# A two-layer hybrid decoder trunk: the four products of the running sums go into one PSUM bank

## The chip, the cores and the metric

The kernel runs on one core of one Trainium2 chip. The metric is the device time of one execution in microseconds (us); lower is better. The engines are TensorE (PE in the profile; PEld is its weight load), VectorE (DVE), ScalarE (ACT), GpSimd (POOL) and SyncE (SP). Matrix products are written to PSUM, here eight banks of 128 x 512 float32, and are read from there by VectorE or ScalarE.

## The reference, cut to what matters

Two layers; 256 tokens, width 1024, everything float32. Each layer normalises the stream, multiplies it with one combined input weight, runs three token mixers side by side, projects and gates each, adds them, and applies one output projection.

```python
for layer in range(2):
    h = rms_norm(x, norm_w[layer])
    proj = jnp.einsum('bsd,de->bse', h, w_in[layer])
    (a_xbc, a_z, a_dt, b_q, b_k, b_v, b_z,
     c_q, c_k, c_v, c_f, c_z, gates) = jnp.split(proj, split_at, axis=-1)
    y_a = mamba2_branch(a_xbc, a_z, a_dt, ...)              # state space, 16 heads in 4 groups
    y_b = sliding_window_branch(b_q, b_k, b_v, b_z, ...)    # 16 heads, window 128
    y_c = forgetting_attention_branch(c_q, c_k, c_v, c_f, c_z, ...)
    branch = jnp.einsum('bsiw,iwd->bsid', jnp.stack([y_a, y_b, y_c], axis=2), w_proj[layer])
    g = jax.nn.sigmoid(gates.reshape(b, s, 3, d) + gate_bias[layer])
    x = x + jnp.einsum('bsd,de->bse', jnp.sum(g * branch, axis=2), w_out[layer])
return rms_norm(x, final_norm_w)
```

Two of the mixers need running sums over the tokens, and these are what the change touches:

```python
# state space: dt = softplus(dt_raw + dt_bias), a = -exp(a_log)
a_cum = jnp.cumsum(a_dt, axis=-1)                       # within each chunk of 128 tokens
seg = a_cum[..., :, None] - a_cum[..., None, :]
decay = jnp.where(causal, jnp.exp(jnp.where(causal, seg, 0.0)), 0.0)
# forgetting attention
log_f = jax.nn.log_sigmoid((f_logit + f_bias).astype(jnp.float32))
cum = jnp.transpose(jnp.cumsum(log_f, axis=1), (0, 2, 1))  # over all 256 tokens
sc = sc + cum[:, :, start:end, None] - cum[:, :, None, :end]
```

## The kernel before

**Dense products.** Every projection multiplies float32 numbers as a high part and a low part (`hi`, `lo`): three products per block of 128, high by high, low by high, high by low. The activations are split once. The weights come from DRAM on SyncE's queue into `raw` tiles of 128 x 1024, ScalarE copies the high part (L291) and VectorE subtracts for the low part (L292), one tile after the other, all the way through a layer. A projection's PSUM tile is evicted by ScalarE (L490, L491 and others) and the partial sums are added by GpSimd's accumulating transfer (L492) or by VectorE. All matrix products and transposes pass through two helpers, so the profile shows them under L107 and L111.

**PSUM.** Three of the eight banks form the pool `mm` (`pmm()`, L77), mainly for projections, five the pool `mx` (`pmx()`, L80), for everything else: scores, transposes, values, decays, running sums. A pool hands its banks out in a fixed rotation; whoever gets a bank waits until the last reader of its former content is done.

**Order.** The kernel's text is generated by a small planner: projections are the main stream, and the mixers are generators that are pumped between projections. A generator yields a number (microseconds of TensorE work until it is due) or a condition. The planner's order is the order in which each engine's queue receives its instructions; every engine runs its queue in order. Transfers of weights are issued on SP's queue, those of running sums on ScalarE's queue, the accumulating ones on GpSimd's.

**The sliding-window quads** (`attn_quad` with `window=True`, four heads at a time). Each takes four banks of `mx` for its scores. VectorE masks and finds the maximum of the first block (L619), ScalarE exponentiates (L614), then the second block: VectorE L627, L628, L632, ScalarE L614 reading PSUM directly. Then the denominators (L638 to L643), transposes of the probabilities `pp`, the copies L677, L679 and L680, and the products with the values, whose bank VectorE reads at L727 when the gate is multiplied in.

**The running sums** (`decay_logits`, L766). When the four logits tiles of a layer are there, it computes softplus and log-sigmoid on VectorE and ScalarE into `rates`, yields until due, and then multiplies with the triangle `tri` of ones:

- one product into a bank `pa` (128 tokens x 32) gives the state-space sums with tokens on partitions; ScalarE copies them to `acum` (L802),
- three products into a second bank `pc` (64 rows x 128 tokens, the last with `ones`, which carries the first chunk's total into the second) give both sums with tokens along the free axis; ScalarE copies them to `cum` (L811), and two transfers on ScalarE's queue (L814) store them in DRAM as `cumd`.

**Who reads the sums.** `cumd` is read back, broadcast to all partitions, by the forgetting attention (`bias`, L1036, then GpSimd's mask L1043) and by each of the four state-space groups (`bcg`, L860, on ScalarE's queue). A state-space group (`ssd_group`) subtracts `acum` (L872, L882), exponentiates on ScalarE (L873, L884, L888), multiplies with the products of B and C (L897) and runs the decay products on TensorE (L901 to L910). The convolution of the state-space input is elementwise: ScalarE L830, three VectorE L833, ScalarE L839, VectorE L840.

Of the kernel before, what the change touches and what calls it, by code (L numbers as in the profile page):

```python
# [13 lines left out]
AF = mybir.ActivationFunctionType  # L14
ALU = mybir.AluOpType

P = 128
# [31 lines left out]
def hybrid_trunk(  # L49
# [17 lines left out]
    def T(tag, shape, dtype=F32, bufs=None):  # L67
        count[0] += 1
        return sb.tile(shape, dtype, tag=tag, name=f"{tag}_{count[0]}",
                       bufs=bufs if bufs is not None else BUFS.get(tag, 1))  # L70

    def PS(tag, bufs):
        count[0] += 1
        return ps.tile([P, 512], F32, tag=tag, name=f"{tag}_{count[0]}", bufs=bufs)
# [4 lines left out]
    def pmx():  # L79
        return PS("mx", 5)  # L80

    act = nc.scalar.activation
# [18 lines left out]
    def mm(o, a, b, **kw):  # L101
        n = b.free_size()
        if a.dtype == F32R:
            clock["t"] += max(0.094, n / 2350.0)
        else:
            clock["t"] += max(0.2, n / 587.0) * (0.5 if a.free_size() == 64 or a.shape[0] == 32 else 1.0)
        nc.tensor.matmul(o, a, b, **kw)  # L107
# [82 lines left out]
    tri = T("tri", [P, P])  # L190
# [27 lines left out]
    def bc(ap, axis, n):  # L218
        s = list(ap.shape)
        s.insert(axis, n)  # L220
        return ap.unsqueeze(axis).to_broadcast(s)
# [204 lines left out]
    for l in range(L):  # L426
        y = Layer()
# [328 lines left out]
    def logits(y, t, i, p):  # L756

        if y.u is None:
            y.u = T("u", [P, 2, 32])
        o, b = y.u[:, t, 16 * i:16 * i + 16], y.hb[:, 16 * i:16 * i + 16]  # L760
        tt(o, p, b, op=ALU.add)
        y.logits += 1
        if y.logits == 4:
            launch(1, decay_logits(y), 0.0)

    def decay_logits(y):  # L766
        u = y.u

        tmp = T("L1", [P, 4, 2, 32])
        e = w = tmp[:, 0, :, :]  # L770
        act(e, u, AF.Abs)
        act(e, e, AF.Exp, scale=-1.0)
        s = tmp[:, 1, :, :]
        ts(s, e, 2.0, None, op0=ALU.add)
        nc.vector.reciprocal(s, s)
        tt(s, s, e, op=ALU.mult)
        s2 = tmp[:, 2, :, :]
        tt(s2, s, s, op=ALU.mult)
        q = tmp[:, 3, :, :].rearrange("p t c -> p (t c)")
        s2f = s2.rearrange("p t c -> p (t c)")  # L780
        sf = s.rearrange("p t c -> p (t c)")
        ts(q, s2f, 1.0 / 19.0, None, op0=ALU.mult)
        for m in (17, 15, 13, 11, 9, 7, 5, 3):
            stt(q, q, 1.0 / m, s2f, op0=ALU.add, op1=ALU.mult)  # L784
        stt(q, q, 1.0, sf, op0=ALU.add, op1=ALU.mult)
        q3 = q.rearrange("p (t c) -> p t c", t=2)
        y.dt = T("dt", [P, 2, 16])
        rates = T("rates", [P, 2, 2, 16])
        lf = tmp[:, 2, :, 0:16]
        ts(w[:, :, 0:16], u[:, :, 0:16], 0.0, 0.5, op0=ALU.max, op1=ALU.mult)  # L790
        tt(y.dt, w[:, :, 0:16], q3[:, :, 0:16], op=ALU.add)
        ts(y.dt, y.dt, 2.0, None, op0=ALU.mult)
        ts(w[:, :, 16:32], u[:, :, 16:32], 0.0, 0.5, op0=ALU.min, op1=ALU.mult)
        tt(lf, w[:, :, 16:32], q3[:, :, 16:32], op=ALU.subtract)
        ts(rates[:, :, 0, :], lf, -16.0, None, op0=ALU.mult)
        tt(rates[:, :, 1, :], y.dt, bc(y.nega, 1, 2), op=ALU.mult)
        yield D_CUM

        pa = pmx()
        mm(pa[:, 0:32], tri, rates[:, :, 1, :], start=True, stop=True)  # L800
        y.acum = T("acum", [P, 2, 16])
        act(y.acum, pa[:, 0:32].rearrange("p (t c) -> p t c", t=2), AF.Copy)  # L802


        pc = pmx()
        for c in range(2):
            mm(pc[32 - 32 * c:64 - 32 * c, 0:P], rates[:, c, :, :].rearrange("p w c -> p (w c)"), tri,
               start=True, stop=(c == 0))
        mm(pc[0:16, 0:P], rates[:, 0, 0, :], ones, start=False, stop=True)
        cum = T("L1", [64, P])  # L810
        act(cum, pc[0:64, 0:P], AF.Copy)  # L811
        y.cumd = dr.tile([2, 16, S], F32, name=f"cumd{y.l}", tag=f"cumd{y.l}")
        for c in range(2):
            nc.scalar.dma_start(y.cumd[:, :, c * P:(c + 1) * P].rearrange("w c s -> (w c) s"),  # L814
                                cum[32 - 32 * c:64 - 32 * c, :])
# [586 lines left out]
    with tc.manual_schedule(engines={ENG.PE, ENG.DVE, ENG.Activation, ENG.Pool}):  # L1402
# [11 lines left out]
        p = pmx()  # L1414
# [151 lines left out]
```

## Time and profile before

| | |
|---|---|
| median of 3 runs | 824.98 us (824.52 to 825.41) |
| the profiled execution | 824.13 us, of it 822.3 in the profile's span |
| granted TensorE clock, mean over the span | 0.994 |
| bytes moved | 170.35 MB, 207 GB/s on average |

How to read the lines that follow. The page gives for each engine its busy time, its share of the span and its instructions. A line of the waits reads: engine, tile and line that waited, what released it, then total us, count, mean us. A line of the timeline reads: start, duration, engine, line, operation, output <- inputs, sizes, count (several alike are merged into one line; the duration then is that of all of them), and in brackets the idle time ahead of it with what ended it. A line of the stretches reads: from and to, length, then for PE, PEld, DVE, ACT and POOL the busy us with the instructions that started, the granted TensorE clock (1.00 is full), the busy share of the 16 DMA engines, GB/s. Layer 0 lies roughly in the first half of the span, layer 1 in the second, and the running sums are formed at 118 to 125 and 511 to 518 us.

### The profile page before, as it was taken

The page shows a single profiled execution, that of the slowest core. Times are in us where ns is not written, and L with a number is a line of the kernel's source. Part 1 is how long each engine was busy: PE and PEld are TensorE (multiplying, and loading weights), DVE is VectorE, ACT ScalarE, POOL GpSimd, SP SyncE. Part 2 cuts the span into 40 slices and gives each one's busy share as a digit, 9 for nine tenths or more (in the row PEclk, how much of TensorE's full clock was granted, in tenths as well). Part 3 has the DMA queues.
Part 4 walks back from the last instruction along what each step waited for, and adds up shares of the span by engine and source line. Part 5 has one row for each costly group of instructions (what it writes and reads, how often), then busy time and mean ns, then how long its engine had stood idle before and what let it go on. Part 6 is the DMA issues. An engine that isn't in the chain of part 4 may idle for free.

```text
span 822.3 us, 14971 instructions
## 1 busy us (share of the span) xinstructions
PE 806.2 (98%) x5198; PEld 719.4 (87%) x5198; DVE 675.8 (82%) x1452; ACT 539.6 (66%) x1168; POOL 163.6 (20%) x233
## 2 busy tenths in 40 slices
PE   9999989999999999999999998999999999999996
PEld 8998968988888888888999897888888889888896
DVE  6878898979999797855786989897989877887665
ACT  7777767865776778543666776786557767684452
POOL 3066113120210111030005711302103110102100
PEclk9999999999999999999999999999999999999999
DMA  9898887688865554866689878668977556468632
GB/s 315 277 252 186 229 230 180 191 234 230 256 205 164 163 151 149 273 206 206 216 269 263 200 217 227 182 186 229 276 227 206 148 174 172 140 203 271 204 103 77
DMA packets 138708, 170.35 MB, mean 207 GB/s; under 512 B 9346, under 2 KB 106362, under 8 KB 138634
## 3 DMA queue, kind: packets, MB, share of 16 engines
q1 hardware_dynamic: 114960, 140.53, 55.2%
q0 software_dynamic: 12928, 12.63, 9.4%
q10 hardware_dynamic: 10746, 16.24, 6.4%
q8 instruction: 41, 0.67, 0.3%
q14 instruction: 33, 0.27, 0.1%
HBM read 154.63 MB, written 2.16 MB: 191 GB/s over the span
## 4 chain that ended last, share of the span: by engine, by line
PE 90%; DVE 6%; ACT 2%; issue 1%; DMA 0%; ACTq 0%; DVEq 0%
PE mm L107 80%; PE mx L107 7%; PE mx L111 4%; DVE lo L292 2%; DVE L L833 2%; ACT pp L614 1%; ACT hi L291 0%; DVE pp L619 0%; DMA L<-in_x_dram 0%; DVE pp L643 0%; DVE L L784 0%; DVE mx L627 0%; DVE L L727 0%; DVE L L840 0%; DVE L L680 0%
## 5 line engine op out<-in xcount | busy, mean ns | idle before, releaser
L107 PE MATMUL mm<-L,hi 128*128 128x512 f32 x1056 | 357.0, 389 | 0.0
L292 DVE TENSOR_TENSOR lo<-raw,hi 128x1024 fp32r<-128x1024 f32 (+2 forms) x276 | 312.0, 1149 | 53.8 <-ACT hi L291 50.9
L107 PE MATMUL mm<-hi,L 128*128 128x512 f32 (+2 forms) x1232 | 322.9, 351 | 0.1
L291 ACT ACTIVATE hi<-raw 128x1024 fp32r<-128x1024 f32 (+2 forms) x276 | 265.1, 981 | 63.3 <-PE mm L107 53.1
L107 PE MATMUL mm<-L,lo 128*128 128x256 f32 x1056 | 268.1, 274 | 0.0
L107 PEld LDWEIGHTS mm<-hi,L 128*128 128x128 f32 x1232 | 217.2, 190 | 24.0 <-issue 1.3
L107 PEld LDWEIGHTS mm<-L,hi 128*128 128x128 f32 x1056 | 196.2, 191 | 27.2 <-issue 4.1
L107 PE MATMUL mm<-lo,L 128*128 128x512 f32 (+2 forms) x616 | 213.6, 348 | 0.0
L107 PEld LDWEIGHTS mm<-L,lo 128*128 128x128 f32 x1056 | 203.7, 193 | 5.5
L107 PEld LDWEIGHTS mm<-lo,L 128*128 128x128 f32 x616 | 116.3, 190 | 11.7 <-DVE lo L292 0.2
L492 POOL DMA_DIRECT2D L<-L x68 | 59.5, 888 | 198.8 <-ACT L L491 132.3
L490 ACT ACTIVATE L<-mm 128x256 f32<-128x256 f32 x84 | 31.9, 379 | 25.9 <-PE mm L107 22.8
L833 DVE SCALAR_TENSOR_TENSOR L<-L,vec,L 128x255 f32<-128x255 f32 (+2 forms) x96 | 46.2, 481 | 2.0 <-ACT L L830 0.3
L1043 POOL TENSOR_SCALAR_AFFINE_SELECT bias<-bias 128x128 f32<-128x128 f32 x64 | 28.1, 476 | 87.4 <-DMA bias<-cumd 60.6
L1077 ACT ACTIVATE L<-L 128x512 f32<-128x512 f32 x24 | 15.1, 629 | 30.4 <-DVE L L1074 25.9
L656 ACT ACTIVATE pp<-pp,nm 128x128 f32<-128x128 f32 x64 | 28.2, 442 | 9.9 <-DVE nm L650 9.9
L492 POOL DMA_DIRECT2D qt<-L x16 | 13.8, 860 | 88.1 <-ACT qt L491 41.3
L614 ACT ACTIVATE pp<-pp,nm 128x128 f32<-128x128 f32 x32 | 12.6, 393 | 24.9 <-DVE nm L619 24.1
L964 POOL TENSOR_TENSOR sm<-sm,mhalf 128x4 f32<-128x4 f32 x8 | 9.9, 1241 | 88.0 <-DVE sm L961 88.0
L491 ACT ACTIVATE L<-mm 128x256 f32<-128x256 f32 x68 | 25.9, 380 | 1.0 <-DMA L<-L 1.0
L1122 POOL TENSOR_TENSOR L<-L,L 128x512 f32<-128x512 f32 x8 | 12.8, 1598 | 67.1 <-DVE L L1121 67.1
L928 ACT ACTIVATE L<-L 128x256 f32<-128x256 f32 x48 | 19.8, 413 | 9.3 <-DVE L L483 9.1
(210 smaller groups left out, 871.1 us busy)
## 6 DMA issues: line engine op xcount, KB each, us to landing
raw<-in_w_in_dram SPq DMA_DIRECT2D x191, 512.0 KB, 4.6
raw<-in_w_proj_dram SPq DMA_DIRECT2D x48, 512.0 KB, 5.5
L<-L POOLq DMA_DIRECT2D x72, 128.0 KB, 5.0
raw<-in_w_out_dram SPq DMA_DIRECT2D x16, 512.0 KB, 4.7
bias<-cumd ACTq DMA_DIRECT2D x16, 256.0 KB, 3.5
L<-cumd ACTq DMA_DIRECT2D x8, 512.0 KB, 5.8
L<-in_gate_bias_dram ACTq DMA_DIRECT2D x12, 256.0 KB, 4.5
qt<-L POOLq DMA_DIRECT2D x16, 128.0 KB, 5.2
```

The source lines that it names most:

```text
L107: nc.tensor.matmul(o, a, b, **kw)
L111: nc.tensor.transpose(o, a, i)
L291: keep(act)(hi, src, AF.Copy)
L292: keep(tt)(lo, src, hi.bitcast(F32), op=ALU.subtract)
L490: act(halves(lo), ordered(p[:, S:2 * S]), AF.Copy)
L491: last = act(halves(out), ordered(p[:, 0:S]), AF.Copy)
L492: nc.gpsimd.dma_start(out, lo, accum_op=ALU.add)
L614: act(pps[b][:, h // 2, h % 2 * P:h % 2 * P + P], of, AF.Exp, scale=0.125 if b else -1.0, bias=nm[:, e:e + 1], accum_out=sums[:, e:e + 1])
L656: act(pp[:, i, sl], pp[:, i, sl], AF.Exp, scale=-1.0, bias=nm[:, e:e + 1], accum_out=sums[:, e:e + 1])
L833: stt(a[:, s:S], x_[:, 0:S - s], y.vec[:, 16 * j + u:16 * j + u + 1], a[:, s:S], op0=ALU.mult, op1=ALU.add)
L928: act(th, o, AF.Tanh, scale=0.5)
L1043: nc.gpsimd.affine_select(out=bias[:, i, dst], in_=bias[:, i, src], compare_op=ALU.is_ge, fill=NEG, base=0, pattern=[[-1, P]], channel_mul ...
```

## The change

Only `decay_logits` changes. The pool `mx` is asked for one bank instead of two. The product for `acum` goes to the columns 128 to 159 of the bank whose columns 0 to 127 take the products for `cum`. ScalarE's copy to `acum` is written behind the last of the four products.

```diff
-        pa = pmx()
-        mm(pa[:, 0:32], tri, rates[:, :, 1, :], start=True, stop=True)
-        y.acum = T("acum", [P, 2, 16])
-        act(y.acum, pa[:, 0:32].rearrange("p (t c) -> p t c", t=2), AF.Copy)
-
-
         pc = pmx()
+        mm(pc[:, P:P + 32], tri, rates[:, :, 1, :], start=True, stop=True)
         for c in range(2):
             mm(pc[32 - 32 * c:64 - 32 * c, 0:P], rates[:, c, :, :].rearrange("p w c -> p (w c)"), tri,
                start=True, stop=(c == 0))
         mm(pc[0:16, 0:P], rates[:, 0, 0, :], ones, start=False, stop=True)
+        y.acum = T("acum", [P, 2, 16])
+        act(y.acum, pc[:, P:P + 32].rearrange("p (t c) -> p t c", t=2), AF.Copy)
         cum = T("L1", [64, P])
         act(cum, pc[0:64, 0:P], AF.Copy)
```

## The prediction

> **What bounds the kernel now.** I read the page first, for the engine that sets the end, then the list of who TensorE waited for, then the timeline and the stretches around its one long wait.
>
> ```profile
> span 822.3 us, 14971 instructions
> PE 806.2 (98%) x5198; PEld 719.4 (87%) x5198; DVE 675.8 (82%) x1452; ACT 539.6 (66%) x1168; POOL 163.6 (20%) x233
> ```
>
> TensorE works 806.2 of 822.3 us. Only 16.1 us are not its own work, so a gain can come from that remainder or from a faster clock. The waits of TensorE put half of the remainder in one place, twice, once per layer:
>
> ```profile
> PE mx L107 <- ACT pp L614: 8.0, 2, 4.0
> ...
> 118.36 0.30 PE L107 MATMUL mx<-rates,tri 128*128 128x32 f32 x2
> 122.18 0.37 ACT L614 ACTIVATE pp<-mx,nm 128x128 f32<-128x128 f32 x1 [0.40 <-DVE nm L632]
> 122.69 0.41 PE L107 MATMUL mx<-tri,rates 128*32 128x128 f32 x4 [4.02 <-ACT pp L614]
> 515.70 0.41 PE L107 MATMUL mx<-tri,rates 128*32 128x128 f32 x4 [4.03 <-ACT pp L614]
> ...
> 118.40:122.70 4.30, 0.28 (x5) 0.17 (x3) 4.23 (x21) 2.28 (x11) 0.00 (x0) 1.00 0.70 211
> 123.50:126.90 3.40, 3.40 (x12) 2.94 (x12) 3.24 (x8) 2.83 (x10) 0.86 (x1) 0.50 0.25 37
> ```
>
> These are exactly the products of the change. The product for `acum` (tile `pa`) runs at 118.36. The next one, for `cum` (tile `pc`), stands still until 122.69, because `pc` gets the bank of the first score of the running sliding-window quad, and L614's second-block exponential reads that bank until 122.55. TensorE's queue is in order, so everything behind it stands too. In the stretch 118.40 to 122.70 TensorE is busy 0.28 of 4.30 us and VectorE 4.23: VectorE is doing that quad's softmax and does not wait for TensorE. The last row shows a second cost: for 3.40 us after the wait the granted clock is 0.50.
>
> **The change, part by part.** It asks the `mx` pool once instead of twice. All four products then go into the bank that `pa` has now, and every later `mx` tile takes a bank one place earlier in the rotation of five, so one that was given back earlier or at the same time. The instructions and their order on each engine stay the same, transfers included; only the copy to `acum` falls behind the `pc` products, directly ahead of the copy to `cum`, and that is where ScalarE runs it in any case:
>
> ```profile
> 116.81 0.68 DVE L727 SCALAR_TENSOR_TENSOR L<-mx,L 128x512 f32<-128x512 f32 x1
> 117.81 0.68 DVE L727 SCALAR_TENSOR_TENSOR L<-mm,L 128x512 f32<-128x512 f32 x1
> 123.52 0.69 DVE L643 TENSOR_TENSOR pp<-pp,rsum 128x512 f32<-128x512 f32 x1
> 125.08 0.22 ACT L802 ACTIVATE acum<-mx 128x32 f32<-128x32 f32 x1
> 125.16 0.28 ACT L811 ACTIVATE L<-mx 64x128 f32<-64x128 f32 x1
> ...
> 123.25 0.59 PE L107 MATMUL mm<-L,hi 128*128 128x512 f32 x1
> 130.26 0.60 PE L111 MATMUL mx<-ident,pp 128*128 128x128 f32 x4
> 130.62 0.46 PE L107 MATMUL mm<-L,hi 128*128 128x512 f32 x1
> 135.94 0.60 PE L111 MATMUL mx<-ident,pp 128*128 128x128 f32 x4
> 516.43 0.80 PE L107 MATMUL mm<-L,hi 128*128 128x512 f32 x1
> 523.23 0.60 PE L111 MATMUL mx<-ident,pp 128*128 128x128 f32 x4
> ```
>
> *The wait.* The bank taken is free when the first L727 ends, 117.49, before `pa`'s product starts. So 4.02 and 4.03 us go. The projections behind start at 118.66 + 0.56 (122.69 to 123.25) = 119.22; the `mm` bank that the second L727 releases is back at 118.49. The next thing that could be late is the transposes of `pp`: they follow two projections later and need L643, which is done at 124.21.
>
> *The clock.* The two projections after the wait take 123.25 to 130.26 = 7.01 us; the next two, of the same work, 130.62 to 135.94 = 5.32. The half clock costs 7.01 - 5.32 = 1.69 us in layer 0, and 6.80 - 5.32 = 1.48 in layer 1. With no stand still I take it to go. So the transposes start at 119.22 + 5.32 = 124.54, after L643's 124.21. The Trainium skill ("TensorE: Matmul & The Clock Gate", section "What's actually happening") says that the clock halves after an idle window of about 3.4 us and comes back after as long a busy one; the trace agrees with 4.02 us of wait and 3.40 us at 0.50, and the two 1-2 us waits forecast below would leave the clock alone by it.
>
> *Copies.* `acum` and `cum` are copied at 125.08 and 125.16 although `pa` was done at 118.66: ScalarE has earlier work, which hides the `acum` copy's longer wait. Without that cover it would be 0.56 us late, and nothing reads `acum` before 175. Cost nothing.
>
> TensorE alone would so gain 4.02 + 1.69 + 4.03 + 1.48 = 11.22 us.
>
> **What catches it.** TensorE's operands come from the splits (L291 on ScalarE, L292 on VectorE) and the branches' elementwise work, and VectorE is at 82%. How much earlier does it get? It ran through the wait, so it can win only where it later idled for TensorE:
>
> ```profile
> 126.01 1.06 ACT L291 ACTIVATE hi<-raw 128x1024 fp32r<-128x1024 f32 x1 [0.57 <-PE mm L107]
> 127.84 0.38 ACT L490 ACTIVATE L<-mm 128x256 f32<-128x256 f32 x1 [0.77 <-PE mm L107]
> 130.46 0.38 ACT L490 ACTIVATE L<-mm 128x256 f32<-128x256 f32 x1 [0.41 <-PE mm L107]
> 132.21 1.06 ACT L291 ACTIVATE hi<-raw 128x1024 fp32r<-128x1024 f32 x1 [0.30 <-PE mm L107]
> ...
> 128.84 0.43 DVE L840 SCALAR_TENSOR_TENSOR L<-L,L 128x256 f32<-128x256 f32 x1 [0.51 <-ACT L L839]
> 130.09 1.23 DVE L292 TENSOR_TENSOR lo<-raw,hi 128x1024 fp32r<-128x1024 f32 x1 [0.49 <-ACT hi L291]
> 133.30 1.23 DVE L292 TENSOR_TENSOR lo<-raw,hi 128x1024 fp32r<-128x1024 f32 x1 [1.42 <-ACT hi L291]
> 134.70 1.00 DVE L833 SCALAR_TENSOR_TENSOR L<-L,vec,L 128x255 f32<-128x255 f32 x2 [0.17 <-ACT L L830]
> ...
> 127.00:134.70 7.70, 7.70 (x50) 7.09 (x49) 4.86 (x6) 5.97 (x15) 1.95 (x3) 1.00 0.58 129
> 134.70:167.60 32.90, 32.90 (x227) 28.75 (x227) 31.61 (x66) 24.96 (x59) 8.29 (x12) 1.00 0.81 220
> 520.00:527.67 7.67, 7.67 (x50) 7.07 (x49) 4.87 (x8) 6.36 (x15) 1.97 (x3) 1.00 0.55 122
> ```
>
> ScalarE idled 0.57 + 0.77 + 0.41 + 0.30 = 2.05 us for TensorE up to 132.21, VectorE 0.51 + 0.49 + 1.42 = 2.42 us for ScalarE up to 133.30. With TensorE 5.7 us ahead both run without these gaps. Since each feeds the other I take 2.2, between the two. After 134.70 VectorE has 31.61 us of work in 32.90: it can win at most the other 1.29 there, which is mostly short hand-overs with ScalarE, so I count none of it. Layer 1 has the same picture (4.87 against 4.86 us busy). The bounds for VectorE's lead are therefore 0 (every gap filled by something else) and 2.42 + 1.29 = 3.71.
>
> Where does TensorE meet VectorE? At the decay products of the first state-space group:
>
> ```profile
> 167.57 0.42 ACT L839 ACTIVATE L<-L 128x256 f32<-128x256 f32 x1 [1.65 <-DVE L L833]
> 167.62 0.33 ACTq L860 DMA_DIRECT2D L<-cumd  x1
> 175.13 0.16 DVE L872 TENSOR_TENSOR ds<-L,acum 128x4 f32<-128x4 f32 x1 [4.19 <-DMA L<-cumd]
> 187.67 0.33 ACTq L860 DMA_DIRECT2D L<-cumd  x1
> 192.68 0.16 DVE L872 TENSOR_TENSOR ds<-L,acum 128x4 f32<-128x4 f32 x1 [1.98 <-DMA L<-cumd]
> 193.93 1.88 DVE L897 TENSOR_TENSOR L<-L,mx 128x512 f32<-128x512 f32 x3
> 195.24 1.53 PE L107 MATMUL mx<-L,L 128*64 128x128 f32 x24
> 586.14 1.88 DVE L897 TENSOR_TENSOR L<-L,mx 128x512 f32<-128x512 f32 x3
> 588.21 1.53 PE L107 MATMUL mx<-L,L 128*64 128x128 f32 x24
> ```
>
> The broadcast of L860 is issued at 167.62 behind ScalarE's L839, which waited for VectorE. VectorE then waits for its landing (175.13). The next one is issued at 187.67 and ends at 192.68; its group's three L897 end at 195.81, and TensorE uses the last of them some two thirds into the pass that starts at 195.24, at 196.26. So this chain keeps VectorE's lead of 2.2 and no more, and TensorE may lead it by another 196.26 - 195.81 = 0.45 us. In layer 1: 588.21 + 1.02 - (586.14 + 1.88) = 1.21. TensorE keeps 2.2 + 0.45 = 2.65 us in layer 0 and 2.2 + 1.21 = 3.41 in layer 1, and gives back 5.71 - 2.65 = 3.06 and 5.51 - 3.41 = 2.10 in new waits, some of it possibly at earlier meetings. After each meeting both engines are ahead together and nothing takes it back.
>
> *Sum.* 2.65 + 3.41 = 6.06 us. The profiled execution took 824.13 us (span 822.3 and 1.8 around it), so 818.07; the median of the runs is 824.98, 0.85 above it, so 818.9. With the bounds of VectorE's lead: 2 x 0 + 1.66 = 1.66 gives 823.3, and 2 x 3.71 + 1.66 = 9.08 gives 815.9.
>
> **Rivals.**
>
> *TensorE keeps everything.* The broadcasts land as much earlier as their data exist: `cum` leaves TensorE 4 us sooner, and the transfers of the wait's aftermath move little (share 0.25, 37 GB/s). Then 824.98 - 11.22 = 813.8. Against it: L860's issue at 167.62 waits for VectorE, not for `cum`, and 31.61 of 32.90 leaves VectorE no room for 5.7 us.
>
> *VectorE wins nothing,* 823.3: the gaps of 0.49 and 1.42 could belong to the loads of `raw`, which slow to 37 GB/s just there. Against it, the rows name TensorE as what ScalarE waited for.
>
> *The clock falls again: slower.* TensorE gives back 5.16 us in several new waits. If each of them, though short, halved the clock as the 4.02 us one did, each would cost another 1.6 us (mean of 1.69 and 1.48). From four such waits on the 6.06 is eaten; three a layer give 818.9 + 9.6 = 828.5. The places are the pass at 195.24, that at 588.21 and projections ahead of them that wait for VectorE. For it: the one long wait did cost that. Against: the new ones are under 2 us each, and TensorE works without a gap on either side. The Trainium skill has this rule: in "TensorE: Matmul & The Clock Gate", "A second HAM failure mode: psum-queue depth-cycling", frequent small idles between groups of matmuls keep the clock swinging; no row of this trace shows it for idles of this size.
>
> *The change does not do what it says:* if the shared bank were handed out at `pc`'s place, the wait for L614 would stay and the time be 825.0. The rotation speaks against it: the first request takes the bank of L727.
>
> **How the numbers follow.** The forecast has 0.65, TensorE keeping all 0.17, VectorE winning nothing 0.08, the clock falling again 0.05, no effect 0.05. The predicted time is 818.9. The forecast's own range is 815.9 to 821.3 (half of VectorE's lead lost: 2.2 us). To hold 8 in 10 I take 813.6 to 822.4: it takes in the rival at 813.8 and most of the way to 823.3. What a measurement can tell from no change is about 0.2%, 1.65 us. VectorE winning nothing lies on that bound, so half of it counts as the same: faster 0.65 + 0.17 + 0.04 = 0.86, same 0.09, slower 0.05.
>
> **What would show it.** The wait of `mx` for L614 gone from TensorE's waits; clock 1.00 where the projections follow `cum`'s products; the first transposes of `pp` near 124.5 and 517.7. VectorE's L833 that starts now at 134.70 near 132.5, and its L872 at about 173 instead of 175.13. New TensorE waits of together about 5 us, named after VectorE's L897 or splits, between 150 and 200 and again around 588. It would be wrong if L872 is 5 us earlier (then near 813.8), or not at all (823.3), or if rows at clock 0.50 appear behind the new waits.

## The result, and the profile after

| | before | after |
|---|---|---|
| median | 825.19 us (824.52 to 825.97, 4 runs) | 817.61 us (816.47 to 818.14, 4 runs) |
| ratio, after to before | | 0.9906, 95% interval 0.9889 to 0.9923 |
| profiled execution, its span | 824.13, 822.3 | 816.47, 814.7 |
| mean granted TensorE clock | 0.994 | 0.999 |

The change takes 7.6 us off. The prediction was 818.9 us, 6.1 off; the measured median lies 1.3 us below it. The edit shortens the file by three lines, so L830, L833, L839, L860, L872 and L897 of the text above are L827, L830, L836, L857, L869 and L894 in profiles of the change.

First the page of the changed kernel, and who TensorE waited for. The three numbers of a line of the waits are the total in us, the times, and the longest single wait (not the mean):

```profile
span 814.7 us, 14971 instructions
PE 805.0 (99%) x5198; PEld 717.2 (88%) x5198; DVE 675.2 (83%) x1452; ACT 538.2 (66%) x1168; POOL 162.6 (20%) x233
...
PE mx L111 <- POOL ident masks.py:199: 1.5, 1, 1.5
PE mm L107 <- ACT qt L491: 0.7, 1, 0.7
PE mx L107 <- DVE L L894: 0.5, 2, 0.4
```

The wait for L614 is gone from the list. The work is the same. TensorE's idle time fell from 16.1 to 9.7 us and its busy time, in which the half clock counted, by 1.2. Two new lines are there, for an eviction (L491) and for the decay products (L894), 1.2 us in all.

The timeline and one stretch around the running sums of layer 0, and the sums and the next transposes in layer 1:

```profile
118.48 0.30 PE L107 MATMUL mx<-rates,tri 128*128 128x32 f32 x2
118.72 0.41 PE L107 MATMUL mx<-tri,rates 128*32 128x128 f32 x4
124.62 0.60 PE L111 MATMUL mx<-ident,pp 128*128 128x128 f32 x4
...
506.81 0.30 PE L107 MATMUL mx<-rates,tri 128*128 128x32 f32 x2
507.05 0.41 PE L107 MATMUL mx<-tri,rates 128*32 128x128 f32 x4
512.95 0.60 PE L111 MATMUL mx<-ident,pp 128*128 128x128 f32 x4
...
119.20:124.60 5.40, 5.40 (x34) 4.92 (x33) 5.09 (x26) 4.06 (x21) 0.00 (x0) 1.00 0.42 129
```

All four products run in one go, the projections behind them at clock 1.00. From the first product for `cum` to the transposes of `pp` it is now 124.62 - 118.72 = 5.90 us, and in layer 1 the same. Before it was 130.26 - 122.69 = 7.57 and 523.23 - 515.70 = 7.53: the half clock had cost 1.67 and 1.63.

Then the places at which VectorE's chain ties TensorE down. These are VectorE's convolution at the point where it had stopped idling, ScalarE's issues of the broadcast, and VectorE's first use of it:

```profile
132.27 1.00 DVE L830 SCALAR_TENSOR_TENSOR L<-L,vec,L 128x255 f32<-128x255 f32 x2
165.17 0.33 ACTq L857 DMA_DIRECT2D L<-cumd  x1
171.85 0.17 DVE L869 TENSOR_TENSOR ds<-L,acum 128x4 f32<-128x4 f32 x1 [3.36 <-DMA L<-cumd]
184.40 0.33 ACTq L857 DMA_DIRECT2D L<-cumd  x1
188.16 0.17 DVE L869 TENSOR_TENSOR ds<-L,acum 128x4 f32<-128x4 f32 x1 [0.72 <-DMA L<-cumd]
...
553.47 0.33 ACTq L857 DMA_DIRECT2D L<-cumd  x1
561.10 0.16 DVE L869 TENSOR_TENSOR ds<-L,acum 128x4 f32<-128x4 f32 x1 [4.30 <-DMA L<-cumd]
578.00 0.16 DVE L869 TENSOR_TENSOR ds<-L,acum 128x4 f32<-128x4 f32 x1 [1.29 <-DMA L<-cumd]
```

VectorE's lead in layer 0 is 134.70 - 132.27 = 2.43 us, and the issue has the same lead, 167.62 - 165.17 = 2.45. Up to here it is close to the forecast 2.2. But then L869 is 175.13 - 171.85 = 3.28 us early, and the second one 192.68 - 188.16 = 4.52. The broadcasts landed faster: issue to use 6.68 us in place of 7.51, and 3.76 in place of 5.01.

TensorE's own lead can be read off at four points (before against after): transposes of layer 0, 130.26 against 124.62, 5.64 us; first product of the sums in layer 1, 511.38 against 506.81, 4.57; transposes there, 523.23 against 512.95, 10.28; the whole execution, 824.13 against 816.47, 7.66. So layer 0 won 5.64 and gave back 1.07; layer 1 won 5.71 and gave back 2.62. The row of before for 511.38:

```profile
511.38 0.30 PE L107 MATMUL mx<-rates,tri 128*128 128x32 f32 x2
```

TensorE's instructions and their order are the same in the two kernels, so its lead can be followed product by product. It falls at four places in each layer: at a bank that VectorE's L1071 reads, at one that VectorE's L727 reads, at one that ScalarE's L491 evicts, and at the decay products behind L894. The two large falls are in layer 1. Its rows, of the changed kernel, and under them the row of before that belongs to 563.13 (the lead falls there from 571.46 - 561.80 = 9.66 at the transposes ahead of it to 571.81 - 563.13 = 8.68):

```profile
561.29 0.21 ACT L870 ACTIVATE ds<-ds 128x4 f32<-128x4 f32 x1 [3.04 <-DVE ds L869]
561.80 0.60 PE L111 MATMUL mx<-ident,L 128*128 128x128 f32 x4
563.13 0.48 PE L107 MATMUL mm<-L,hi 128*128 128x512 f32 x1 [0.73 <-ACT qt L491]
579.99 1.04 PE L107 MATMUL mx<-L,L 128*64 128x128 f32 x12 [0.36 <-DVE L L894]
581.19 0.88 PE L107 MATMUL mx<-L,L 128*64 128x128 f32 x12 [0.16 <-DVE L L894]
```

```profile
571.46 0.60 PE L111 MATMUL mx<-ident,L 128*128 128x128 f32 x4
571.81 0.46 PE L107 MATMUL mm<-L,hi 128*128 128x512 f32 x1
```

The first row shows that ScalarE, too, stood 3.04 us for the first reader of the broadcast (its exponential of `ds`), and its evictions with it.

### The profile page after: what moved, and what is told of

It is laid out like the page before. It is cut to its first block, busy times and chain, and to the rows that moved or that the text cites. A ratio compares the mean times of both kernels' runs of the same rounds, so it can differ in the third digit from the quotient of the medians.

```text
span 814.7 us, 14971 instructions
## 1 busy us (share of the span) xinstructions
PE 805.0 (99%) x5198; PEld 717.2 (88%) x5198; DVE 675.2 (83%) x1452; ACT 538.2 (66%) x1168; POOL 162.6 (20%) x233
## 4 chain that ended last, share of the span: by engine, by line
PE 81%; DVE 10%; DMA 3%; ACT 3%; issue 3%; ACTq 0%; DVEq 0%
PE mm L107 72%; PE mx L107 6%; PE mx L111 3%; DVE lo L292 3%; DMA L<-cumd 3%; DVE L L830 2%; ACT hi L291 1%; ACT pp L614 0%; DVE L L292 0%; ACT L L827 0%; DVE pp L643 0%; DVE L L894 0%; DMA L<-in_x_dram 0%; DVE pp L619 0%; DVE L L679 0%
## 5 line engine op out<-in xcount | busy, mean ns | idle before, releaser
L830 DVE SCALAR_TENSOR_TENSOR L<-L,vec,L 128x255 f32<-128x255 f32 (+2 forms) x96 | 46.2, 481 | 1.7
L614 ACT ACTIVATE pp<-pp,nm 128x128 f32<-128x128 f32 x32 | 12.6, 394 | 23.5 <-DVE nm L619 22.7
L491 ACT ACTIVATE L<-mm 128x256 f32<-128x256 f32 x68 | 25.9, 381 | 0.7 <-DMA L<-L 0.7
```

The source lines that it names most:

```text
L491: last = act(halves(out), ordered(p[:, 0:S]), AF.Copy)
L830: stt(a[:, s:S], x_[:, 0:S - s], y.vec[:, 16 * j + u:16 * j + u + 1], a[:, s:S], op0=ALU.mult, op1=ALU.add)
```

## The experiments

The question after the result was what took back 3.7 of the 11.35 us that TensorE won, and whether the half clock was a cost of its own. The theory: VectorE, standing still for the landing of the broadcast with splits queued behind it. The main rival: VectorE's own work, or ScalarE's evictions, hold TensorE in any case.

**The wait of VectorE taken away.** In the change and, beside it, in the kernel before, the first reader of the broadcast is held behind the last of the `xdt` products (L866 in the changed kernel, L869 in the kernel before):

```diff
-            tt(xdt[:, t, :].rearrange("p (h d) -> p h d", h=4),
+            ready = tt(xdt[:, t, :].rearrange("p (h d) -> p h d", h=4),
...
-        tt(ds, bcg[:, :, P - 1], y.acum[:, 0, hs], op=ALU.subtract)
+        with tc.issue_after(ready.ins): tt(ds, bcg[:, :, P - 1], y.acum[:, 0, hs], op=ALU.subtract)
```

> The change, with VectorE's first reader of the broadcast (the subtraction into ds, L869) held behind L866, some 10 us later in VectorE's queue; TensorE's order is the same. Theory that VectorE stands still for the broadcast's landing with splits queued behind it, and that this is what takes back the rest of TensorE's lead: VectorE's waits for the broadcast (3.4, 0.7, 4.3 and 1.3 us) go, TensorE's lost lead behind 163 us and 554 us (1.0 and 2.4 us) mostly with them, and the time is 814 to 815.5. Rival, that VectorE's own work or ScalarE's evictions hold TensorE: the waits go or move and the time stays at 817 to 818.

> The kernel before with the same late L872. Theory: there TensorE was not held by VectorE behind its long wait (no wait for L897 or for a split in its trace), so VectorE's freedom is worth nothing: 825 us, within 0.2%. Rival, that VectorE's wait for the broadcast already cost time in the kernel before: 822 to 823.

> The change once more, beside the next two on the same chip: 817.6 us. The landing of the first group's broadcast (issue to L869's start) was 6.7 us in layer 0 and 7.6 in layer 1; if such times vary from execution to execution, they differ here by up to 1 us, and the time with them.

Measured on one chip: the change again 816.80 us (816.17 to 816.98, 4 runs; ratio 0.9892, 0.9876 to 0.9909), the change with the late reader 814.94 (814.76 to 814.97; ratio 0.9871, 0.9857 to 0.9886), the kernel before with the late reader 825.56 against 825.34 (ratio 1.0005, 0.9996 to 1.0015). In the timeline of the change with the late reader, L869 stands without a bracket, so it waits for no landing, and TensorE's two new waits of the changed kernel have left its list. The first row is of the timeline, the rest are TensorE's waits:

```profile
178.25 0.25 DVE L869 TENSOR_TENSOR ds<-L,acum 128x4 f32<-128x4 f32 x1
...
PE mx L111 <- POOL ident masks.py:199: 1.5, 1, 1.5
PE mx L111 <- DMA L<-in_x_dram: 0.5, 1, 0.5
PE mm L107 <- DVE L L1071: 0.2, 1, 0.2
```

In the same stretch of 40 us in layer 1, VectorE gets from 33.72 to 37.04 us of work and TensorE from 38.72 to 39.97. The row of the changed kernel comes first:

```profile
546.00:586.00 40.00, 38.72 (x239) 32.91 (x238) 33.72 (x60) 23.84 (x47) 8.80 (x13) 1.00 0.88 245
```

```profile
546.00:586.00 40.00, 39.97 (x249) 34.68 (x248) 37.04 (x68) 25.87 (x49) 9.22 (x13) 1.00 0.93 267
```

The same edit brings 1.9 us behind the change and nothing in the kernel before, where TensorE had no wait for a split or a decay product to lose. This version is also the fastest of all. TensorE's lead over the profiled execution of before shows where the gain lies. In the table stands how much of it is lost at each of the four places, layer 0 and layer 1, in us (lines of the changed kernel):

| place | the change | the change again | the change, late reader |
|---|---|---|---|
| bank read by VectorE L1071 | 0.36, 0.33 | 0.38, 0.33 | 0.39, 0.28 |
| bank read by VectorE L727 | 0.30, 0.30 | 0.30, 0.29 | 0.29, 0.29 |
| bank evicted by ScalarE L491 | 0.06, 0.99 | 0.51, 0.77 | 0, 0 |
| decay products behind L894 | 0.36, 0.98 | 0.91, 0.38 | 0, 0 |

So the theory holds for the larger part: the losses at L491 and L894, 2.4 to 2.6 us, go with the wait for the landing. The other 1.3 us are lost in all three, at banks that VectorE's own work frees late; for them the rival is right.

**The half clock alone.** The time in which TensorE stands still is filled with useless products; nothing else changes. The second kernel has `range(8)`:

```diff
         mm(pa[:, 0:32], tri, rates[:, :, 1, :], start=True, stop=True)
+        for _ in range(17):
+            nc.tensor.matmul(pa[:, P:2 * P], tri, ident, start=True, stop=True)
```

> The kernel before with 17 more products of tri and ident, written into unused columns of pa's bank, in the time in which TensorE waits for L614 (about 3.7 of 4.0 us filled). Theory that the clock falls because TensorE stands still: granted clock 1.00 behind the wait, the two projections there in 5.3 us instead of 7.0, and since 1.7 and 1.5 us of lead are less than TensorE could keep, all of it in the time: about 822.0 us. Rival, that the half clock costs nothing in the end because VectorE is not ahead: about 825. If the clock falls for another reason than the idle time: 0.50 stays and 825.

> As filled_wait, with 8 products in place of 17: they take about 1.9 us (17 took 4.0), so TensorE stands still for about 2.1 us. If the clock falls only behind a stand still nearly as long as the 4.0 us one, it stays 1.00 and the time is that of filled_wait, about 821.5. If 2 us are enough, 0.50 stands behind the wait and the time is 824 to 825.

Filled: 821.46 us against 824.55 (821.09 to 821.77, 5 runs; ratio 0.9961, 0.9947 to 0.9975). The timeline shows the products, the `cum` product at its old place, and the stretch behind it at full clock:

```profile
118.57 4.04 PE L802 MATMUL mx<-ident,tri 128*128 128x128 f32 x34
122.75 0.41 PE L107 MATMUL mx<-tri,rates 128*32 128x128 f32 x4
...
123.30:126.90 3.60, 3.60 (x23) 3.33 (x23) 3.39 (x10) 2.65 (x12) 0.86 (x1) 1.00 0.23 32
```

So the wait itself is still paid, but the half clock behind it is not: 3.1 us, close to the 1.67 + 1.63 = 3.30 that it cost in the profile. The clock fell because TensorE stood still, and its cost reaches the time in full.

Half filled gave no single answer: 823.06 us (821.90 to 824.97, 10 runs; ratio 0.9979, 0.9970 to 0.9989). The profiled execution, the fastest, kept the clock in both layers. Its timeline and the stretch behind the wait:

```profile
123.49 0.41 PE L107 MATMUL mx<-tri,rates 128*32 128x128 f32 x4 [2.15 <-ACT pp L614]
...
123.00:126.50 3.50, 3.01 (x21) 2.60 (x22) 3.19 (x13) 3.24 (x16) 0.86 (x1) 1.00 0.16 56
```

Two other executions of it had a mean clock of 0.994, as the kernel before has, and 824.67 and 824.97 us. By these mean clocks a stand still of 2.15 us sometimes costs the clock and sometimes not; no fallen execution of this kernel was profiled.

**Which reader holds the bank.** In the kernel before, the product for `acum` takes a bank of the other pool:

```diff
-        pa = pmx()
+        pa = pmm()
```

> The kernel before with pa's product in a bank of the pool mm, so that cum's products get the bank of L727 without a wait. Theory that only the last reader of the bank counts: the wait for L614 goes, but every projection gets a later bank of mm: the second one behind the products needs the bank of the projection ahead of them, which ScalarE evicts only at 124.0 to 124.4 (L490, L491), and would wait from about 122.0, 2.4 us, in each layer. If the clock holds through that, TensorE is 1.6 + 1.7 us ahead behind it, less than VectorE lets it keep: about 818.5 to 819; if it falls, 1.6 us, about 822. Rival, that two banks at that place cost the 4 us whichever pool gives them: 825.

820.02 us against 824.67 (819.82 to 821.31, 4 runs; ratio 0.9942, 0.9926 to 0.9959). The wait for L614 is gone, and the forecast wait for the eviction is there, in both layers. Behind the second one the clock fell:

```profile
124.82 0.48 PE L107 MATMUL mm<-L,hi 128*128 128x512 f32 x1 [2.40 <-ACT L L491]
514.76 0.48 PE L107 MATMUL mm<-L,hi 128*128 128x512 f32 x1 [2.43 <-ACT L L491]
...
123.00:126.50 3.50, 1.68 (x10) 1.57 (x11) 3.19 (x11) 3.50 (x15) 0.86 (x1) 1.00 0.04 13
515.00:519.00 4.00, 4.00 (x16) 3.47 (x16) 3.93 (x8) 3.92 (x10) 1.74 (x2) 0.59 0.28 42
```

Two banks do not cost 4 us by themselves. What costs is the last reader of the bank that one gets. The time lies between the two cases expected, as the clock fell in one layer of the profiled execution and held in the other.

**The rotation.** The change, and one more bank asked for behind the shared one and left unused:

```diff
+        pmx()
         cum = T("L1", [64, P])
```

> The change, with one bank of the mx pool asked for and left unused behind the shared one, so that every later tile gets the bank that it had before. Theory that the shared bank alone is the gain: 817.6 us, as the change. Rival, that the later tiles' earlier banks carry part of it: between 818.5 and 825, with new waits for L614 or L643 in front of the transposes of pp.

816.83 us (816.63 to 817.18, 4 runs; ratio 0.9903, 0.9888 to 0.9918), by its ratio as the change (0.9906 and 0.9892). The later tiles' earlier banks are worth nothing that can be measured.

**One layer at a time.** The edit is the change under `if y.l == 0:` or `if y.l == 1:`, with the old lines in the other branch.

> One shared bank in layer 0, two banks in layer 1. The trace of the change puts 4.6 us of the gain in layer 0: about 820.6 us against 825.2 before. If layer 0 is worth what the prediction's step gave it (2.65 us), 822.5. In layer 1 the wait of 4.0 us for L614 and the half clock behind it stay.

> Two banks in layer 0, one shared bank in layer 1. The trace of the change puts 3.1 us there: about 822.1 us. The prediction's step gave 3.41 us: 821.8. If the two layers' gains depend on each other, the two single gains do not add up to 7.6 us.

Layer 0 alone: 821.13 us (820.59 to 821.31, 4 runs; ratio 0.9954, 0.9939 to 0.9969), 3.4 us off. Layer 1 alone: 821.39 (820.79 to 821.66; ratio 0.9957, 0.9942 to 0.9972), 3.2 off. The two make 6.6 us, against 7.7 for both together on the same chip (824.55 - 816.83, of the kernel with the old rotation, as the change itself did not run there). The profiles show one reason: in the layer that keeps the wait, the clock stayed low for longer than in the profiled execution of before. The first pair of lines is layer 1 of the one kernel, the second pair layer 0 of the other:

```profile
511.79 0.64 PE L107 MATMUL mx<-tri,rates 128*32 128x128 f32 x4 [4.01 <-ACT pp L614]
520.19 0.60 PE L111 MATMUL mx<-ident,pp 128*128 128x128 f32 x4
```

```profile
123.08 0.64 PE L107 MATMUL mx<-tri,rates 128*32 128x128 f32 x4 [4.02 <-ACT pp L614]
131.40 0.60 PE L111 MATMUL mx<-ident,pp 128*128 128x128 f32 x4
```

That is 8.40 and 8.32 us, against 5.90 at full clock: 2.50 and 2.42 us lost to the clock, where before lost 1.63 and 1.67. Without these extra 0.87 and 0.75 us TensorE's lead in the two profiles is 4.4 us for layer 0 alone and 4.0 for layer 1 alone. The kernel before with the late reader had a longer one still in its layer 0, 131.69 - 122.96 = 8.73, so 2.83 us:

```profile
122.96 0.64 PE L107 MATMUL mx<-tri,rates 128*32 128x128 f32 x4 [4.02 <-ACT pp L614]
131.69 0.60 PE L111 MATMUL mx<-ident,pp 128*128 128x128 f32 x4
```

Which part of the gain belongs to which layer is therefore not fixed to better than about 1 us.

**How long the broadcasts take.** From nine profiled executions, the time from ScalarE's issue to VectorE's use, for the broadcasts of the first and the third group of each layer (VectorE waited for the landing in each; the second group's is issued right behind the first):

| kernel | layer 0 | layer 1 |
|---|---|---|
| before | 7.51, 5.01 | 7.86, 3.86 |
| the change | 6.68, 3.76 | 7.63, 4.33 |
| the change again | 7.14, 4.30 | 7.39, 3.74 |
| old rotation | 6.92, 3.93 | 7.39, 3.88 |
| layer 0 only | 6.82, 3.56 | 6.54, 4.01 |
| layer 1 only | 6.44, 4.02 | 7.44, 3.57 |
| filled wait | 6.54, 4.56 | 8.11, 3.98 |
| half filled | 7.20, 4.59 | 8.05, 3.59 |
| `acum` in `mm` | 6.95, 4.86 | 6.64, 3.80 |

In layer 0 the profiled execution of before had the longest of each kind. The kernel with layer 1 alone changed is the kernel before in its layer 0, and it has 6.44 and 4.02 there. So a shorter landing needs no change. Over the nine executions a landing varies by 0.8 to 1.6 us, between the two executions of the change by 0.2 to 0.6. The kernel before was profiled once, so whether its 7.51 and 5.01 are usual for it stays open.

What a landing does to the time can be followed in the three executions with both layers changed. VectorE's lead over before at the third group's L894, and TensorE's lead behind the decay products that need it:

| kernel | layer 0: VectorE, TensorE | layer 1: VectorE, TensorE |
|---|---|---|
| the change | 4.52, 4.56 | 6.89, 7.68 |
| the change again | 3.31, 3.34 | 6.50, 7.30 |
| old rotation | 3.71, 3.75 | 6.74, 7.53 |

TensorE keeps what VectorE has, and 0.04 us more in layer 0 and 0.8 more in layer 1, each time.

## Why the prediction was right, step by step

- *The wait goes, nothing takes its place there.* Right: 4.02 and 4.03 us are gone, and the next transposes start at 124.62 (forecast 124.54). The late copy to `acum` cost nothing: ScalarE runs it at 125.20, with the copy to `cum` right behind it, as before:

```profile
125.20 0.21 ACT L806 ACTIVATE acum<-mx 128x32 f32<-128x32 f32 x1
125.27 0.27 ACT L808 ACTIVATE L<-mx 64x128 f32<-64x128 f32 x1
```

- *The clock.* Right, and shown alone by the filled wait. The size of 1.69 and 1.48 was that of one execution; other profiles show up to 2.83. TensorE's win of 11.35 us against the forecast 11.22 agrees.
- *VectorE's lead of 2.2 us.* Right: 2.43 in layer 0; in layer 1 the issue leads by 560.59 - 553.47 - 4.57 = 2.55, where 560.59 stands in the first row below, from the timeline of before.

```profile
560.59 0.33 ACTq L860 DMA_DIRECT2D L<-cumd  x1
584.89 0.16 DVE L872 TENSOR_TENSOR ds<-L,acum 128x4 f32<-128x4 f32 x1 [0.84 <-DMA L<-cumd]
```

- *The chain at L872 ties TensorE to VectorE.* Right in mechanism: TensorE's lead behind the decay products follows VectorE's in three executions, and with the wait for the landing away, 816.80 becomes 814.94. That is 10.4 us below the kernel before on the same chip, against the 11.2 of the rival in which TensorE keeps everything.
- *"So this chain keeps VectorE's lead of 2.2 and no more."* This is the step that was mis-sized, in layer 0. It held the landings at 7.51 and 5.01 us. They took 6.68 and 3.76, so VectorE led by 4.52 at the second, and TensorE kept 4.57 us in place of 2.65. The same kernel profiled again had 7.14 and 4.30, and TensorE kept 3.34 there. In layer 1 the second landing was longer than before, 4.33 against 3.86: VectorE kept 584.89 - 578.00 - 4.57 = 2.32 and TensorE 7.66 - 4.57 = 3.09 (forecast 3.41). Together it is 7.66 against 6.06 in the profiled executions. That the total came this near is in part luck: the two layers erred in opposite directions, and the landings of one execution decided by how much.
- *TensorE may lead VectorE by another 0.45 us in layer 0, and by 1.21 in layer 1.* Both too large: it was 0.04 and 0.79. The last of the three L897 is needed earlier than two thirds into the pass: the wait for it in layer 1 stands in front of the second twelve of the 24 products (581.19 in the rows above), so half way. In layer 0 of before that product starts at 195.95, not at 196.26.
- *The clock does not fall again.* Right for this change: all eight of its executions have a mean clock of 0.997 to 0.999. The row against that rival was thinner than it looked, since waits of 2.15 to 2.43 us did bring the clock down in some executions. The new waits stayed below 1 us each. The Trainium skill ("TensorE: Matmul & The Clock Gate", section "A second HAM failure mode: psum-queue depth-cycling") has frequent small idles between groups of matmuls make the clock swing; with the few waits of at most 0.73 us here, the mean clock of 0.997 to 0.999 does not show it.
- *New waits of about 5 us in all.* Too many: 3.7 us of lead were given back, and the list names 1.2 of them. Idle time without the two long waits rose from 16.1 - 8.05 to 9.7, so by 1.65; busy time fell by 1.2 where the half clock alone was worth 3.3, so the other 2.1 us lie in what the trace counts as busy. The largest single wait was for ScalarE's L491, which the prediction did not name.
- *The signs.* The transposes of layer 0 (124.62, forecast 124.5) and L833 (132.27, forecast 132.5) came as said, L872 at 171.85 was earlier than the 173 forecast. The 517.7 for the transposes of layer 1 is 523.23 less layer 1's own 5.51: it leaves out the lead that layer 0 keeps, which the sum has. Measured: 512.95.

## What to carry to other kernels

When a tile from a rotating pool makes the critical engine wait, look up who reads its bank last; sharing a bank that is already free can remove the wait, while a bank from another pool can bring the next one's reader (here 2.4 us). Before counting a removed wait in full, find what the engines that did not wait feed into the critical one further on: here a third of the win was given back, the larger part where VectorE stood still for a transfer with other work queued behind it, and moving that one reader back brought half of it home. A step whose price is the landing of a transfer needs a range from several executions, not the figure of one.

## What the runs showed of the hardware that was not expected

The half clock behind a wait of 4.0 us cost between 1.63 and 2.83 us in the five places named above, in the same code. The stretches show why. In the kernel before the clock stayed at 0.50 for 3.4 us (123.50 to 126.90 in the prediction's row). It stayed there twice as long, 6.8 us, in the two kernels with one layer changed and in layer 0 of the kernel before with the late reader. These are the rows of the kernel with layer 0 alone changed, in its layer 1, from the moment at which TensorE stops (511.79 - 4.01 = 507.78):

```profile
507.78:510.21 2.43, 0.00 (x0) 0.00 (x0) 2.40 (x10) 1.09 (x5) 0.00 (x0) 1.00 0.49 140
510.21:517.04 6.83, 5.25 (x20) 4.21 (x21) 5.69 (x23) 4.98 (x21) 0.87 (x1) 0.50 0.37 93
517.04:520.00 2.96, 2.96 (x20) 2.73 (x20) 1.79 (x3) 2.21 (x5) 0.87 (x1) 1.00 0.23 46
```

The half clock begins here 2.43 us after TensorE stopped, while it still waits. In the kernel before it begins 0.81 us behind the end of the wait (122.69). Behind waits of 2.15, 2.40 and 2.43 us the clock fell in some executions and held in others: in the kernel with `acum` in the other pool it held in layer 0 (1.00 after 2.40 us) and fell in layer 1 (0.59 on average over the next 4 us, after 2.43 us), in the same execution.

The Trainium skill ("TensorE: Matmul & The Clock Gate", section "What's actually happening") says that the clock is decided by windows of about 3.4 us that run freely, and that the moment of the change varies with where in the window the first product lands. Stretches of 3.4 and 6.8 us at half clock, one and two such windows, fit that, and so does their varying start. It also has the clock halve after an idle window of that length; here a wait of 2.43 us was enough, and the measurement decides.
